# Hybrid decoder block on one core: the attention's scaling of probabilities moved in among the next unit's scores, one more bank for the first unit's transposes

## Chip, core and metric

The kernel runs on one core of one Trainium2 chip. The metric is the device time of one execution in microseconds (us); the median of three runs stands for a kernel. The trace and the profile page come from one further execution, taken by the hardware profiler.

## What is computed

One decoder layer over 512 tokens of width 1024, in float32: a pre-norm, one wide input projection, two mixers (a sparse-attention mixer with 8 query heads in 2 groups, and a recurrent mixer), gates, an output projection with a residual, and a gated feed-forward part. The change lies in the attention mixer alone. Its core is this, cut from the reference:

```python
q = rmsnorm(q.reshape(b, s, G, R, dh), q_norm_g) * (dh ** -0.5)      # G=2 groups, R=4 heads each, dh=64
s_c = einsum('bsgrd,bcgd->bgrsc', q, kc) + bias_c                    # compressed branch: 31 blocks
p_c = masked_softmax(s_c, dist_c >= 0);  o_cmp = einsum('bgrsc,bcgd->bsgrd', p_c, vc)
# selected branch (all blocks up to the token's own are chosen here) and window branch, each:
p = masked_softmax(einsum('bqgrd,bkgd->bgrqk', q, k) + bias, mask);  o = einsum('bgrqk,bkgd->bqgrd', p, v)
gt = sigmoid(gate)
o = gt[..., 0:1] * o_cmp + gt[..., 1:2] * o_slc + gt[..., 2:3] * o_win
```

## The kernel before

Ahead of the attention stage come the projections and the recurrent mixer, behind it the merge, the output projection and the feed-forward part. All dense products are float32 split into a high and a low part, three TensorE passes each (`whi` and `wlo` are the parts of a weight tile, 128x512 moving columns per matmul).

The attention stage works through twelve **units** `(qt, g, bs)`: a tile of 128 queries, a group of four heads, and one or both of the two branches. Units 0 to 3 are query tile 3 (512 keys a head), units 4 to 7 tile 2 (384 keys); each has one branch and four heads. Units 8, 9 (tile 1, 256 keys) and 10, 11 (tile 0, 128 keys) have both branches, so eight rows of scores. For each unit there are these steps:

- `scores(u, n)`: TensorE computes scores of the heads into the two PSUM banks of `pa()` (two matmuls a head, `KH` and `KL`), VectorE adds the bias, negates and takes the minimum on the way into SBUF tile `P` (line 1160, called a **read** below since it frees the bank), ScalarE takes the exponential in place and its sum into `sm`. Between the banks stand `n` **filler** matmuls of a dense projection (`filler`), which have nothing to do with the unit. At the end of the function stands the **scaling**: VectorE turns `sm` into gate over sum, and each head's `P` is multiplied by it, heads 0 to 2 on VectorE (`ts`), head 3 on ScalarE.
- `turns(u)`: groups of four 128x128 transposes of `P` on TensorE (line 1186) into a PSUM bank, called a **turn** here. Banks rotate: two of `pb()` and `tb3` (its tile name is `ps_mm`). `evac` copies each bank to `PTs`, turns with even numbers on ScalarE, odd ones on VectorE (line 1107).
- `compressed(qt)`: the compressed branch for a query tile: eight short matmuls into a `pa()` bank, softmax in `sC` on VectorE and ScalarE. `compressed_t(qt)` transposes `sC` (two transposes into a `pa()` bank, line 1138), ScalarE copies it back.
- `values(u)`: TensorE multiplies `sC` and `PTs` by the values into bank `Ob`, the bank of head sums; for the unit that completes a group ScalarE and VectorE split the result into `oaT`.

TensorE's order in this stage is the written one (`manual_schedule` for TensorE). The orders of VectorE and ScalarE are set by the scheduler of the tile framework when the kernel is built, those of GpSimd (POOL) and the DMA queue SP too. Every engine runs its own list in order, and an instruction that waits holds all behind it. The driving loop keeps scores two units ahead of the transposes:

```python
scores(units[0], 12); compressed(3); scores(units[1], 12)
for i, u in enumerate(units):
    turns(u)
    if i in (0, 4, 8, 10): compressed_t(u[0])
    if i + 2 < len(units): scores(units[i + 2], nfill[i])
    ...
    values(u)
```

Dense weights come by DMA, ScalarE makes `whi`, and in this stage GpSimd makes most `wlo` tiles (line 298, 128x512); a GpSimd subtraction starts when the filler's pass over the older `wlo` tile has ended.

Of the kernel before, what the change touches and what calls it, by code (L numbers as in the profile page):

```python
# [22 lines left out]
NT = S // 128  # L23
# [58 lines left out]
def hybrid_block(ctx: ExitStack, tc: tile.TileContext, A: dict, out: bass.AP):  # L82
# [25 lines left out]
    def bank(tag, bufs, shape=(128, 512)):  # L108
        return ps.tile(list(shape), F32, name="ps_" + tag, tag=tag, bufs=bufs)

    def mmb():
        return bank("mm", 4)

    def pa():
        return bank("a", 2)

    def pb():
        return bank("b", 2)

    def mm(o, l, r, start, stop):  # L120
        te.matmul(o, lhsT=l, rhs=r, start=start, stop=stop)  # L121

    def act(o, i, f=AF.Copy, **kw):
        sc.activation(o, i, f, **kw)  # L124

    def tt(o, a, b, op):
        v.tensor_tensor(o, a, b, op=op)  # L127

    def ts(o, a, s1, s2, op0=ALU.mult, op1=ALU.add):
        if s2 is None:  # L130
            v.tensor_scalar(o, a, s1, None, op0=op0)
        else:
            v.tensor_scalar(o, a, s1, s2, op0=op0, op1=op1)
# [25 lines left out]
    for name in ("rwkv_mu", "rwkv_w0", "rwkv_a0", "rwkv_k_k", "rwkv_k_a", "rwkv_r_k", "rwkv_ln_g", "rwkv_ln_b"):  # L159
        r0, n = ROWS[name]  # L160
# [46 lines left out]
    def norm_tiles(pool_):  # L207
        return (cp.tile([128, NT, 2], F32, name="ss", tag="ss"),
                [pool_.tile([128, D], F32, name="h", tag="h", bufs=NT) for _ in range(NT)])
# [101 lines left out]
    _, hs = norm_tiles(xp)  # L311
# [16 lines left out]
    with tc.manual_schedule(engines={getattr(mybir.EngineType, e) for e in ("PE", "Activation", "DVE", "Pool")}):  # L328
# [10 lines left out]
        for t in range(NT):  # L339
# [9 lines left out]
            if t == 1:  # L349
                pt = pts[7][:, 384:512]  # L350
# [5 lines left out]
        r0, n = ROWS["rwkv_mu"]  # L356
# [26 lines left out]
    def run(g):  # L383
        while True:
            try:
                next(g)
            except StopIteration as e:
                return e.value
# [226 lines left out]
    for k in range(31):  # L615
        m, n = 31 - k, k + 1
# [71 lines left out]
    pt = pa()  # L688
# [370 lines left out]
    Ob, db, tb3 = mmb(), [mmb(), mmb()], mmb()  # L1059
# [29 lines left out]
    def filler(n):  # L1089
        for _ in range(n):  # L1090
            next(fill, None)

    oaT = m2.tile([128, 2, NH2, S], F32R, name="oaT", tag="QK")
    ev, tn = [0], [0]
    Ps, PTk = {}, {}
# [5 lines left out]

    def evac(pt):
        PT = PTs[:, ev[0] % 8]
        if ev[0] % 2 == 0:
            act(PT, pt)
        else:
            v.tensor_copy(PT, pt)
        ev[0] += 1
        return PT

    def compressed(qt):
        qs = slice(128 * qt, 128 * qt + 128)
        pc = pa().rearrange("p (j g e a n) -> p j g e a n", j=2, g=2, e=2, a=2)
        for h in range(H):
            g, j, e = h // 4, h // 2 % 2, h % 2
            mm(pc[:, j, g, e], qst[:, h, qs], KC[:, g], True, True)
        sC = sC2[:, qt % 2]
        mx = at.tile([128, H], F32, name="mx", tag="mx", bufs=2)
        pcs = pc.rearrange("p j g e a n -> p (j g e) a n")
        tt(sC, pcs[:, :, 0], BC.rearrange("p j g e n -> p (j g e) n")[:, :, 24 - 8 * qt:56 - 8 * qt], ALU.add)  # L1120
        tt(sC, sC, pcs[:, :, 1], ALU.add)
        v.tensor_reduce(mx, sC, axis=AX.X, op=ALU.max)
        tt(sC, sC, mx[:, :, None].to_broadcast([128, H, 32]), ALU.subtract)
        act(sC, sC, AF.Exp)
        if qt == 0:
            tt(sC, sC, cmask[:, None, :].to_broadcast([128, H, 32]), ALU.mult)
        v.tensor_reduce(mx, sC, axis=AX.X, op=ALU.add)
        ts(mx, mx, 1e-30, None, op0=ALU.max)
        v.reciprocal(mx, mx)
        mxv = mx.rearrange("p (j g e) -> p j g e", j=2, g=2)  # L1130
        tt(mxv, mxv, gts[:, qt].rearrange("p (g j e x) -> p j g e x", g=2, j=2, e=2)[:, :, :, :, 0], ALU.mult)
        tt(sC, sC, mx[:, :, None].to_broadcast([128, H, 32]), ALU.mult)

    def compressed_t(qt):
        sC = sC2[:, qt % 2]
        pt = pa()
        for j in range(2):
            te.transpose(pt[:, 128 * j:128 * j + 128], sC[:, 4 * j:4 * j + 4].rearrange("p h n -> p (h n)"), ident)  # L1138
        act(sC.rearrange("p h n -> p (h n)"), pt[:, 0:256])

    def scores(u, n):
        qt, g, bs = u
        qs = slice(128 * qt, 128 * qt + 128)
        N = 128 * (qt + 1)
        R = 4 * len(bs)
        P = Pb[units.index(u) % 4][:, 0:R * N].rearrange("p (r n) -> p r n", n=N)
        nm = at.tile([128, 8], F32, name="nm", tag="nm", bufs=2)
        sm = at.tile([128, 8], F32, name="sm", tag="sm", bufs=2)
        per = 4 // (qt + 1)
        nb = R // per  # L1150
        for i0 in range(0, R, per):
            sp = pa()
            for i in range(i0, i0 + per):
                h, b = 4 * g + i % 4, bs[i // 4]
                o = sp[:, N * (i - i0):N * (i - i0) + N]
                mm(o, qst[:, h, qs], KH[:, b, g, 0:N], True, False)
                mm(o, qst[:, h, qs], KL[:, b, g, 0:N], False, True)
            for i in range(i0, i0 + per):
                h = 4 * g + i % 4
                v.tensor_tensor_reduce(out=P[:, i], in0=sp[:, N * (i - i0):N * (i - i0) + N], in1=BT[:, h, 384 - 128 * qt:512],  # L1160
                                       scale=-1.0, scalar=-NEG, op0=ALU.add, op1=ALU.min, accum_out=nm[:, i:i + 1])
                act(P[:, i], P[:, i], AF.Exp, scale=-1.0, bias=nm[:, i:i + 1], accum_out=sm[:, i:i + 1])
            ib = i0 // per
            filler(n * (ib + 1) // nb - n * ib // nb)
        v.reciprocal(sm[:, 0:R], sm[:, 0:R])
        for x, b in enumerate(bs):
            tt(sm[:, 4 * x:4 * x + 4], sm[:, 4 * x:4 * x + 4], gts[:, qt, 12 * g + 1 + b:12 * g + 12:3], ALU.mult)
        for i in range(R):
            if i % 4 == 3:
                act(P[:, i], P[:, i], AF.Copy, scale=sm[:, i:i + 1])  # L1170
            else:
                ts(P[:, i], P[:, i], sm[:, i:i + 1], None)
        Ps[u] = P

    def turns(u):
        qt, g, bs = u
        P = Ps.pop(u)
        PTk[u] = []  # L1180
        for x in range(len(bs)):
            for k in range(qt + 1):
                pt = tb3 if tn[0] % 3 == 2 else pb()
                tn[0] += 1
                for i in range(4):
                    te.transpose(pt[:, 128 * i:128 * i + 128], P[:, 4 * x + i, 128 * k:128 * k + 128], ident)  # L1186
                PTk[u].append((bs[x], k, evac(pt)))

    def values(u):
        qt, g, bs = u  # L1190
        qs = slice(128 * qt, 128 * qt + 128)
        O = Ob[:, 256 * g:256 * g + 256]
        if bs[0] == 0:
            sCT = sC2[:, qt % 2].rearrange("p h n -> p (h n)")
            for j in range(2):
                for e in range(2):
                    mm(O[64 * e:64 * e + 64, 128 * j:128 * j + 128], vcb[:, 2 * g + e], sCT[:, 128 * j:128 * j + 128],
                       j == 0, False)
        for b, k, PT in PTk.pop(u):
            for r in range(2):  # L1200
                mm(O[64 * r:64 * r + 64].rearrange("p (a q) -> p a q", a=2), vt[:, k, b, 64 * g:64 * g + 64],
                   PT.rearrange("p (h q) -> p h q", h=4)[:, r::2, :], False, b == 1 and k == qt)
        if bs[-1] == 1:
            ov = O.rearrange("p (a q) -> p a q", a=2)
            act(oaT[:, 0, 2 * g:2 * g + 2, qs], ov)
            tt(oaT[:, 1, 2 * g:2 * g + 2, qs], ov, oaT[:, 0, 2 * g:2 * g + 2, qs].bitcast(F32), ALU.subtract)

    units = [(qt, g, (b,)) for qt in (3, 2) for g in range(2) for b in range(2)]
    units += [(qt, g, (0, 1)) for qt in (1, 0) for g in range(2)]
    nfill = [5, 5, 6, 6, 7, 8, 10, 10, 10, 9, 9, 6]  # L1210
    with tc.manual_schedule(engines=KTS):
        scores(units[0], 12)
        compressed(3)
        scores(units[1], 12)
        for i, u in enumerate(units):
            turns(u)
            if i in (0, 4, 8, 10):
                compressed_t(u[0])
            if i + 2 < len(units):
                scores(units[i + 2], nfill[i])  # L1220
            else:
                filler(nfill[i])
            if i in (1, 5, 7):
                compressed({1: 2, 5: 1, 7: 0}[i])
            values(u)
        filler(100)
    dbg("oaT", oaT.bitcast(F32))
# [118 lines left out]
    for hf in range(2):  # L1346
        bo = dense_tok(512, aT[:, 0], aT[:, 1], NF)
        for t in range(NT):
            n = 256 if hf and t == NT - 1 else 512
# [32 lines left out]
```

## Time and profile before

| | |
|---|---|
| runs before (us) | 836.18, 836.18, 836.47; median 836.18 |
| profiled execution's own time | 836.53 us |
| its span, first to last instruction | 834.7 us |
| granted TensorE clock | 0.999 |
| attention stage in the trace | from 300.6 us (first score) to 397.3 us (last fillers) |
| busy over the span | TensorE 99%, VectorE 62%, ScalarE 49%, GpSimd 6% |

How to read it: "busy" of TensorE has modelled ends, so starts are compared with starts below. A row of the timeline reads: start in us, duration in us, engine, line, operation, written tile <- read tiles, shape, count, and in brackets how long the engine sat idle and who ended it. PE is TensorE, PEld its weight load, DVE VectorE, ACT ScalarE, POOL GpSimd. Lines are those of the kernel before.

### The profile page before, as it was taken

What the parts mean: (1) busy time and instruction counts of PE and PEld (TensorE: products, weight loads), DVE (VectorE), ACT (ScalarE), POOL (GpSimd) and SP (SyncE); (2) the same over time, 40 slices, a digit from 0 to 9 for tenths busy, and PEclk for the clock granted to TensorE, in tenths of its full rate; (3) what the DMA queues carried; (4) which work ended last, traced back from release to release, by engine and by line L of the source; (5) the groups of instructions that cost most, each with busy time, mean ns of one, the idle gap of its engine ahead of it and who ended that gap; (6) DMA issues with size and microseconds to landing.
All of it is one profiled execution on the core that took longest, in us unless ns stands there. A gap on an engine that the chain in (4) does not pass through costs nothing.

```text
span 834.7 us, 12900 instructions
## 1 busy us (share of the span) xinstructions
PE 824.0 (99%) x5107; PEld 669.6 (80%) x5107; DVE 515.7 (62%) x1004; ACT 406.7 (49%) x795; POOL 51.4 (6%) x67
## 2 busy tenths in 40 slices
PE   8999999999999999999999999999999999999998
PEld 7777778987777876777888988888888888888886
DVE  5577779964565878787665575566655566322222
ACT  6766655454455777676334454444444444221220
POOL 6100020140000110011000000000000000000000
PEclk9999999999999999999999999999999999999999
DMA  8432222246372310000275033333333332223421
GB/s 242 110 85 61 76 76 77 70 127 185 102 127 77 90 38 14 26 27 26 74 256 163 1 101 101 101 102 96 87 95 101 101 101 98 83 98 114 139 75 51
DMA packets 109400, 78.73 MB, mean 94 GB/s; under 512 B 3877, under 2 KB 98012, under 8 KB 109340
## 3 DMA queue, kind: packets, MB, share of 16 engines
q1 hardware_dynamic: 106800, 73.92, 31.0%
q10 hardware_dynamic: 1196, 2.55, 0.9%
q0 software_dynamic: 1344, 1.45, 0.8%
q8 instruction: 40, 0.66, 0.3%
q14 instruction: 20, 0.16, 0.1%
HBM read 74.56 MB, written 2.29 MB: 92 GB/s over the span
## 4 chain that ended last, share of the span: by engine, by line
PE 53%; DVE 0%; DVEq 0%; issue 0%
PE ps_mm L121 52%; PE ps_a L202 0%; PE ps_b L202 0%; PE ps_a L121 0%; PE ps_b L1186 0%; PE ps_mm L1186 0%; DVE x L127 0%; DVEq L1378 0%; PE ps_a L1138 0%
## 5 line engine op out<-in xcount | busy, mean ns | idle before, releaser
L298 DVE TENSOR_TENSOR wlo<-raw,whi 128x1024 fp32r<-128x1024 f32 (+1 forms) x111 | 131.4, 1185 | 184.4 <-PE ps_mm L121 160.0
L121 PE MATMUL ps_mm<-hh,whi 128*128 128x512 f32 (+1 forms) x624 | 242.4, 391 | 0.6 <-DVE hl L136 0.5
L121 PE MATMUL ps_mm<-hl,whi 128*128 128x512 f32 (+1 forms) x624 | 240.3, 387 | 0.0
L124 ACT ACTIVATE whi<-raw 128x1024 fp32r<-128x1024 f32 (+3 forms) x124 | 123.2, 995 | 159.2 <-PE ps_mm L121 143.4
L121 PE MATMUL ps_mm<-hh,wlo 128*128 128x512 f32 (+1 forms) x624 | 152.1, 384 | 0.0
L121 PEld LDWEIGHTS ps_mm<-hh,whi 128*128 128x128 f32 x624 | 117.3, 188 | 27.4 <-issue 1.0
L121 PEld LDWEIGHTS ps_mm<-hl,whi 128*128 128x128 f32 x624 | 117.3, 188 | 22.9 <-issue 1.0
L121 PEld LDWEIGHTS ps_mm<-hh,wlo 128*128 128x128 f32 x624 | 115.1, 188 | 23.5
L121 PE MATMUL ps_mm<-whi,aT 128*128 128x512 f32 x352 | 84.5, 390 | 0.0
L121 PEld LDWEIGHTS ps_mm<-whi,aT 128*128 128x128 f32 x352 | 65.9, 188 | 14.3 <-issue 0.4
L136 DVE SCALAR_TENSOR_TENSOR cgv<-ps_mm,cw,cgv 128x511 f32<-128x511 f32 (+1 forms) x88 | 65.4, 746 | 1.6
L124 ACT ACTIVATE cgv<-ps_mm,cw 128x512 f32<-128x512 f32 x44 | 34.2, 780 | 23.3 <-PE ps_mm L121 23.2
L121 PE MATMUL ps_mm<-wlo,aT 128*128 128x512 f32 x176 | 44.3, 389 | 0.0
L124 ACT ACTIVATE P<-P,nm 128x512 f32<-128x512 f32 (+3 forms) x64 | 35.3, 553 | 14.9 <-DVE nm L1160 14.9
L124 ACT ACTIVATE aT<-cgv 128x512 fp32r<-128x512 f32 x22 | 13.9, 631 | 56.8 <-DVE cgv L127 56.8
L121 PEld LDWEIGHTS ps_mm<-wlo,aT 128*128 128x128 f32 x176 | 33.0, 188 | 6.9
L124 ACT ACTIVATE cgv<-cgv 128x512 f32<-128x512 f32 x22 | 13.9, 632 | 41.3 <-DVE cgv L136 41.3
L298 POOL TENSOR_TENSOR wlo<-raw,whi 128x512 fp32r<-128x512 f32 (+3 forms) x13 | 20.5, 1573 | 203.5 <-PE ps_mm L121 134.0
L1160 DVE CUSTOM_DVE_ANT_0 P<-ps_a,AB 128x512 f32<-128x512 f32 (+3 forms) x64 | 29.4, 483 | 4.2 <-PE ps_a L121 3.7
L127 DVE TENSOR_TENSOR x<-x,ps_mm 128x512 f32<-128x512 f32 (+1 forms) x17 | 11.0, 654 | 24.1 <-PE ps_mm L121 22.7
L127 DVE TENSOR_TENSOR aT<-cgv,aT 128x512 fp32r<-128x512 f32 x22 | 15.2, 693 | 14.7 <-ACT aT L124 14.7
L124 ACT ACTIVATE QK<-ps_mm 128x64 f32<-128x64 f32 (+5 forms) x56 | 14.9, 310 | 18.3 <-PE ps_mm L121 18.2
(354 smaller groups left out, 1211.4 us busy)
## 6 DMA issues: line engine op xcount, KB each, us to landing
raw<-in_w_up_dram SPq DMA_DIRECT2D x44, 512.0 KB, 3.9
raw<-in_w_in_dram SPq DMA_DIRECT2D x38, 512.0 KB, 3.9
raw<-in_w_down_dram SPq DMA_DIRECT2D x22, 512.0 KB, 3.6
raw<-in_w_out_dram SPq DMA_DIRECT2D x8, 512.0 KB, 3.6
xt<-in_x_dram SPq DMA_DIRECT2D x4, 512.0 KB, 4.1
raw<-in_cmp_w_v_dram SPq DMA_DIRECT2D x4, 512.0 KB, 3.9
raw<-in_w_proj_b_dram SPq DMA_DIRECT2D x8, 256.0 KB, 2.7
raw<-in_w_proj_a_dram SPq DMA_DIRECT2D x8, 256.0 KB, 2.8
```

Of the source, the lines that this page charges most:

```text
L121: te.matmul(o, lhsT=l, rhs=r, start=start, stop=stop)
L124: sc.activation(o, i, f, **kw)
L127: v.tensor_tensor(o, a, b, op=op)
L136: v.scalar_tensor_tensor(o, a, s, b, op0=op0, op1=op1)
L298: eng.tensor_tensor(lo, raw, hi.bitcast(F32), op=ALU.subtract)
L1160: v.tensor_tensor_reduce(out=P[:, i], in0=sp[:, N * (i - i0):N * (i - i0) + N], in1=BT[:, h, 384 - 128 * qt:512], scale=-1.0, scalar=-NEG, ...
```

## The change

Four edits, all in the attention stage:

- **A bank**: the fourth turn of unit 0 (`tn[0] == 3`) goes into `Ob`, which nobody uses at that time; the later turns rotate as before, one place on (`tn[0] - (tn[0] > 3)`).
- **The compressed branch of tile 3**: `compressed(3)` is cut in two. It stops after the two additions that read the bank; the rest is issued after unit 0's turns. `compressed_t(3)` moves from right behind those turns to behind the first score bank of unit 2, and uses `tb3` and not a `pa()` bank.
- **Scaling**: a function of its own, `scale(u)`. For units 1 to 9 it is issued inside the `scores` of the next unit, behind its second bank (`mid`); for units 0, 10 and 11 it stays behind the unit's own scores. In the built program this lets VectorE take the next unit's reads between the multiplications of one unit.
- **Copies shared anew**: turns 3 (unit 0) and 27 (unit 7) are evacuated by ScalarE and not by VectorE; for tile 0 (units 10 and 11) all eight multiplications of a unit are on VectorE and none on ScalarE. 

The built programs show the same instructions in the same order on all engines outside this stage, and the same order on GpSimd and the DMA queue throughout. TensorE has the same instructions in the stage; its order differs at `compressed_t(3)` alone, beside the banks.

```diff
     def evac(pt):
         PT = PTs[:, ev[0] % 8]
-        if ev[0] % 2 == 0:
+        if ev[0] % 2 == 0 or ev[0] in (3,27):
             act(PT, pt)
...
         tt(sC, sC, pcs[:, :, 1], ALU.add)
+        if qt == NT - 1:
+            yield
...
     def compressed_t(qt):
-        pt = pa()
+        pt = tb3 if qt == NT - 1 else pa()
...
-    def scores(u, n):
+    def scores(u, n, mid=()):
...
             filler(n * (ib + 1) // nb - n * ib // nb)
+            if ib < len(mid):
+                mid[ib]()
+        Ps[u] = P, sm
+
+    def scale(u):
+        qt, g, bs = u
+        P, sm = Ps[u]
+        R = 4 * len(bs)
         v.reciprocal(sm[:, 0:R], sm[:, 0:R])
...
         for i in range(R):
-            if i % 4 == 3:
+            if i % 4 == 3 and qt:
                 act(P[:, i], P[:, i], AF.Copy, scale=sm[:, i:i + 1])
             else:
                 ts(P[:, i], P[:, i], sm[:, i:i + 1], None)
...
-                pt = tb3 if tn[0] % 3 == 2 else pb()
+                pt = Ob if tn[0] == 3 else tb3 if (tn[0] - (tn[0] > 3)) % 3 == 2 else pb()
...
+        behind = (1,2,3,4,5,6,7,8,9)
         scores(units[0], 12)
-        compressed(3)
+        scale(units[0])
+        comp = compressed(3)
+        next(comp)
         scores(units[1], 12)
         for i, u in enumerate(units):
             turns(u)
-            if i in (0, 4, 8, 10):
+            if i == 0:
+                run(comp)
+            if i in (4, 8, 10):
                 compressed_t(u[0])
             if i + 2 < len(units):
-                scores(units[i + 2], nfill[i])
+                mid = [lambda: None, functools.partial(scale, units[i + 1])] if i + 1 in behind else [lambda: None, lambda: None]
+                if i == 0:
+                    mid.insert(0, functools.partial(compressed_t, 3))
+                scores(units[i + 2], nfill[i], mid)
+                if i + 2 not in behind:
+                    scale(units[i + 2])
```

More of the change, by code (lines that the diff above doesn't have):

```diff
@@ L1 @@
+import functools
 import itertools
@@ L1172, in scores @@
                 ts(P[:, i], P[:, i], sm[:, i:i + 1], None)
-        Ps[u] = P
     def turns(u):
         qt, g, bs = u
-        P = Ps.pop(u)
+        P, _ = Ps.pop(u)
         PTk[u] = []
@@ L1223, in hybrid_block @@
             if i in (1, 5, 7):
-                compressed({1: 2, 5: 1, 7: 0}[i])
+                run(compressed({1: 2, 5: 1, 7: 0}[i]))
             values(u)
```

## Prediction, made before the changed kernel ran

> **What bounds the kernel now.** I read the page first, then the busy time by stretches, then TensorE's timeline through the attention stage, and last VectorE, ScalarE and GpSimd at each place where TensorE waits.
>
> ```profile
> PE 824.0 (99%) x5107; PEld 669.6 (80%) x5107; DVE 515.7 (62%) x1004; ACT 406.7 (49%) x795; POOL 51.4 (6%) x67
> 476.33 354.54 PE ps_mm L121 x1584
> 300.60:397.30 96.70, 93.44 (x647) 72.41 (x645) 79.01 (x278) 68.77 (x192) 10.30 (x8) 1.00 0.08 23
> 312.50:318.80 6.30, 4.89 (x26) 3.10 (x24) 6.09 (x18) 5.04 (x13) 0.62 (x1) 1.00 0.14 42
> ```
>
> TensorE is busy 99%. The second line, a piece of the chain of waits, is TensorE alone for the last 354.54 us: what the attention stage gains or loses arrives at the end one to one. The change removes no TensorE work (same instructions, one order altered), so it can only move TensorE's idle time. The third line is the stage (length, then busy time of PE, PEld, DVE, ACT, POOL): 96.70 - 93.44 = 3.26 us idle. The fourth shows where most lies: 6.30 - 4.89 = 1.41 us around unit 0's turns, where VectorE is busy 6.09 of 6.30 us. Ends are modelled, so idle time is understated; below I compare starts.
>
> **Place A, units 0 to 2: a gain of 1.28 us.** TensorE, then GpSimd and VectorE:
>
> ```profile
> 311.55 1.03 PE L1186 MATMUL ps_b<-kc,P 128*128 128x128 f32 x8
> 312.42 0.60 PE L1186 MATMUL ps_mm<-kc,P 128*128 128x128 f32 x4
> 313.80 0.66 PE L1186 MATMUL ps_b<-kc,P 128*128 128x128 f32 x4 [0.78 <-DVE PTs L1107]
> 314.57 0.44 PE L1138 MATMUL ps_a<-kc,sC 128*128 128x128 f32 x2
> 315.54 0.44 PE L121 MATMUL ps_a<-KH,qst 128*128 128x512 f32 x1
> 316.96 0.50 PE L121 MATMUL ps_a<-KH,qst 128*128 128x512 f32 x1 [0.52 <-DVE nm L1160]
> 318.78 0.66 PE L121 MATMUL ps_mm<-sC,kc 128*64 128x128 f32 x8
> ...
> 311.85 1.28 POOL L298 TENSOR_TENSOR wlo<-raw,whi 128x512 fp32r<-128x512 f32 x1 [9.54 <-ACT sC L124]
> 312.23 0.92 DVE L131 TENSOR_SCALAR mx<-mx 128x8 f32<-128x8 f32 x1
> 314.09 0.42 DVE L127 TENSOR_TENSOR sC<-sC,mx 128x256 f32<-128x256 f32 x1
> 314.43 1.27 DVE L131 TENSOR_SCALAR P<-P,sm 128x512 f32<-128x512 f32 x3
> 316.22 0.68 DVE L1160 CUSTOM_DVE_ANT_0 P<-ps_a,AB 128x512 f32<-128x512 f32 x1
> ...
> 331.83 0.16 DVE L131 TENSOR_SCALAR mx<-mx 128x8 f32<-128x8 f32 x1
> ```
>
> Eight transposes take 312.42 - 311.55 = 0.87 us, a turn 0.44. The fourth turn should start at 312.86 and starts at 313.80: it waits for a bank that VectorE (line 1107) has to copy. In `Ob` it waits for nothing, and the turns end at 313.29. Two transposes and a score bank with its filler take 0.97 (314.57 to 315.54), the bank alone so 0.77. It comes first now, and the transposes of `sC` are wanted at 314.06. `sC` isn't ready: its 128x8 step on VectorE took 0.92 us where the same form took 0.16 at 331.83, and ended at 313.15, with GpSimd's 311.85 + 1.28 = 313.13. Nothing in the change moves that, nor the copy behind it; `sC` is final at about 314.46 as before. So the transposes start at 314.5: 0.94 of wait goes, 0.45 comes. Transposes and second bank, 0.97, and 0.1 of restart (the first matmul after a wait lasts 0.50, as at 316.96, where an estimated 0.4 is usual) end at 315.57. The third bank needs VectorE's first read of unit 2. Before, that stood behind three multiplications (1.27 from 314.43) and a copy, at 316.22, and TensorE waited to 316.96. In the new order one multiplication (0.42) and the two small steps on `sm` (0.2) stand ahead: read from 314.97, done 315.65, third bank at 315.68. The way from there to `values` is unchanged, 318.78 - 316.96 = 1.82: 317.50, against 318.78. Bounds: 0.9 if the read comes 0.4 later, 1.73 if `sC` comes when wanted.
>
> The two edits that leave ScalarE one copy more (turn 3, 0.6 us) are free: it copies three banks until 314.6, before `sC` wants it at 314.7. Without that cover the bank `tb3` would go back 0.6 us later, with `values` behind it.
>
> **Place B, units 3 and 4: 0.48 us of it are given back.**
>
> ```profile
> 338.01 0.66 PE L1186 MATMUL ps_b<-kc,P 128*128 128x128 f32 x4
> 332.28 1.29 POOL L298 TENSOR_TENSOR wlo<-raw,whi 128x512 fp32r<-128x512 f32 x1 [19.16 <-PE ps_mm L121]
> 332.92 0.68 DVE L127 TENSOR_TENSOR mx<-mx,gts 128x8 f32<-128x8 f32 x1
> 333.52 0.68 DVE L136 SCALAR_TENSOR_TENSOR AB<-AB,ps_mm 128x512 f32<-128x512 f32 x1
> 334.45 0.55 DVE L1160 CUSTOM_DVE_ANT_0 P<-ps_a,AB 128x384 f32<-128x384 f32 x1
> 336.86 0.62 ACT L124 ACTIVATE P<-P,sm 128x384 f32<-128x384 f32 x1 [0.51 <-DVE sm L127]
> 337.38 0.58 ACT L124 ACTIVATE PTs<-ps_b 128x512 f32<-128x512 f32 x1
> ```
>
> Unit 3's fourth turn (338.01) waits for ScalarE's copy of its first turn (337.38). That stands behind the multiplication of unit 4's head 3 (336.86), and so behind all four reads of unit 4, the third of them at 334.45. This chain doesn't come forward by the whole 1.28 us. GpSimd's span moves with TensorE, to about 331.1 to 332.4; the last step on `sC` (two inputs in SBUF) and the filler step of 0.6 (333.52) are in line before the third read. A step of that kind ran until GpSimd's end at 332.92 (0.68, to 333.60; GpSimd ended at 333.57). So: step on `sC` done 332.7, filler step 333.3, one multiplication of unit 3 that the edit puts here, 0.36, 333.66, third read there: 0.79 earlier than before, with an unchanged tail behind it. TensorE leaves the fourth turn 0.8 us ahead, whatever it was ahead before: a loss of 0.48. Bounds: 0.3 ahead if the step on `mx` too loses to GpSimd (I place it 0.1 us before GpSimd's start); 1.4 if neither waits.
>
> [...]
>
> **Place C, unit 9: a gain of 0.97 us.**
>
> ```profile
> 365.37 1.67 DVE L131 TENSOR_SCALAR P<-P,sm 128x256 f32<-128x256 f32 x6
> 366.95 1.28 DVE L1107 COPY PTs<-ps_b 128x512 f32<-128x512 f32 x2
> 368.15 0.41 DVE L1160 CUSTOM_DVE_ANT_0 P<-ps_a,AB 128x256 f32<-128x256 f32 x1
> 367.33 1.29 POOL L298 TENSOR_TENSOR wlo<-raw,whi 128x512 fp32r<-128x512 f32 x1 [10.96 <-PE ps_mm L121]
> 367.74 0.86 PE L121 MATMUL ps_mm<-obT,whi 128*128 128x512 f32 x3
> 368.97 0.39 PE L121 MATMUL ps_a<-KH,qst 128*128 128x256 f32 x1 [0.37 <-DVE nm L1160]
> 370.26 0.38 PE L121 MATMUL ps_a<-KH,qst 128*128 128x256 f32 x1
> ```
>
> Three fillers from 367.74 end their turn at 368.44, and TensorE starts at 368.97: 0.53 plus 0.1 of restart. The next wait is 0.35 long: 368.97 to 370.26 is 1.29, and four score matmuls at about 0.12 and two fillers at 0.23 make 0.94. VectorE is late: six multiplications and two copies stand before unit 9's first read at 368.15. New, one copy is ScalarE's (turn 27, 0.6) and the sixth multiplication comes behind four reads (0.28). With TensorE 0.8 us ahead the read starts at about 366.6 and is not missed. The fifth multiplication starts at 366.33, GpSimd at 366.5: a margin of 0.2 us.
>
> **Places D and E, units 8 and 9: -0.40 and +0.75 us.**
>
> ```profile
> 373.89 0.66 PE L1186 MATMUL ps_b<-kc,P 128*128 128x128 f32 x4
> 373.64 0.91 ACT L124 ACTIVATE P<-P,sm 128x256 f32<-128x256 f32 x2 [0.17 <-DVE sm L127]
> 374.46 0.36 ACT L124 ACTIVATE oaT<-ps_mm 128x256 fp32r<-128x256 f32 x1
> 374.72 1.33 ACT L124 ACTIVATE PTs<-ps_b 128x512 f32<-128x512 f32 x2
> 375.95 0.41 ACT L124 ACTIVATE sC<-sC 128x256 f32<-128x256 f32 x1
> 383.06 1.04 PE L1186 MATMUL ps_b<-kc,P 128*128 128x128 f32 x8
> 384.89 0.66 PE L1186 MATMUL ps_mm<-kc,P 128*128 128x128 f32 x4 [0.79 <-ACT PTs L124]
> 383.39 0.69 ACT L124 ACTIVATE P<-P,sm 128x128 f32<-128x128 f32 x2 [0.53 <-DVE sm L127]
> 384.25 0.59 ACT L124 ACTIVATE PTs<-ps_mm 128x512 f32<-128x512 f32 x1
> ```
>
> D: unit 8's fourth turn waits for ScalarE's copy of the first. Before, the copy began 0.83 us after the turns (373.89 to 374.72). In the new order ScalarE does `oaT` first, which can start only when `values` of unit 7 ends, 0.1 after the turns begin; then one multiplication (0.45) and the `sC` exponential (0.41), moved ahead; then the copy: 0.1 + 0.26 + 0.45 + 0.41 = 1.2, so 0.4 later. E: unit 9's fourth turn should start at 383.06 + 0.87 = 383.93 and starts at 384.89, 0.96 late: ScalarE copies only at 384.25, behind the two multiplications of unit 10 at 383.39. Those are VectorE's now; ScalarE is free for the copy when unit 10's exponentials end, and 0.2 us of wait are left. The two multiplications cost VectorE 0.4 us more in units 10 and 11, hidden: its next read is wanted 1 us later.
>
> The sum in time saved: 1.28 - 0.48 + 0.97 - 0.40 + 0.75 = 2.1 us. The profiled execution took 836.53, so 834.4 for its like; the median of the runs is 0.35 lower, 836.18, and gives **834.1 us**. No DMA or GpSimd order changes, and the loads have slack in the stage (share 0.08).
>
> **Rivals.** (1) *More is kept* (0.2): places B and D don't bind, because the copies on ScalarE come early enough. Speaks for it that one small step decides B. Then 2.1 + 0.48 + 0.40 = 3.0: 833.2. (2) *The fourth turns eat it* (0.22): each unit of four turns has three banks, so TensorE ahead only waits longer for ScalarE's copy, at C as well as at B; rows 338.01 and 384.89 are such waits already. What is left is the 0.8 at B and about 0.1 behind it, 0.9: 835.3. (3) *The edit does nothing*, the scheduler placing the multiplications where they were: the built order speaks against it, so it has no share of its own beside (2). (4) *Slower* (0.1): multiplications among the reads meet GpSimd's spans (332.28, 367.33, in unit 10 one more of 1.3) and hold the reads queued behind them. The point: a VectorE step in SBUF starting after GpSimd does, 0.1 us later in unit 4, 0.2 in unit 9. Each costs up to 1.3; all three, 3.9, against the 2.1 + 0.7 (B with no wait on `sC`, 1.4 against 0.8) of gain otherwise: 1.1 worse, 837.3.
>
> **How the numbers follow.** The forecast has 0.48. A measurement of this kernel can tell about 0.2% (1.67 us) from no change, so 834.5 is the border of faster. The forecast lies 0.4 beyond it, and its B and D are each uncertain by some 0.5: seven tenths of it (0.34), and all of (1) (0.2), give faster 0.54. Slower by over 0.2% (above 837.85) needs (4) with a further wait, 0.05. The rest, 0.41, is within. The range 832.6 to 836.1 takes in (1) with A's upper bound, and (2) with B's lower one, and leaves (4) out.
>
> **What would show it.** Right: no wait at unit 0's fourth turn; `sC` transposes at about 314.5; unit 3's fourth turn near 337.1 behind ScalarE's copy; no wait for a read in unit 9; the last fillers of the stage 2.1 us earlier. Wrong: VectorE multiplications of over 1 us ending with a GpSimd subtraction and a TensorE wait for a read behind them; or stage gain lost after 397 us.

## The result, and the profile after

The kernel after the change takes **833.82 us** (median of 8 runs, 833.71 to 834.27), against 836.30 us for the kernel before in the same session (836.18 to 836.58): 2.48 us less, a ratio of 0.9971 with a 95% interval of 0.9961 to 0.9980. The profiled execution took 833.78 us with a span of 831.9 us. In the listings of after, lines 121, 124, 127, 131, 136, 298, 1107, 1138, 1160 and 1186 of before are 122, 125, 128, 132, 137, 299, 1108, 1141, 1163 and 1196; in the versions with GpSimd's pieces the lines behind 299 stand two further down.

First the page's busy time, then the busy time by stretches (length, then busy time of PE, PEld, DVE, ACT, POOL; granted clock, DMA share, GB/s):

```profile
PE 823.2 (99%) x5107; PEld 669.9 (81%) x5107; DVE 514.4 (62%) x1006; ACT 406.4 (49%) x793; POOL 51.5 (6%) x67
300.60:395.00 94.40, 92.68 (x646) 72.58 (x645) 77.94 (x280) 68.65 (x190) 10.49 (x8) 1.00 0.09 25
312.50:318.80 6.30, 5.83 (x40) 3.94 (x40) 5.38 (x18) 6.01 (x15) 0.18 (x1) 1.00 0.14 42
```

No engine's busy time has changed by more than 1.3 us. Over the stage TensorE is idle 94.40 - 92.68 = 1.72 us where it was idle 3.26, and in the stretch around unit 0's turns 6.30 - 5.83 = 0.47 us where it was idle 1.41. Three of the four waits that the profile lists for TensorE between 305 and 398 us (engine, tile, line, what it waited for; total us, how often, longest):

```profile
PE ps_mm L1196 <- ACT PTs L125: 0.6, 1, 0.6
PE ps_mm L1141 <- DVE sm L128: 0.5, 1, 0.5
PE ps_b L1196 <- ACT PTs L125: 0.2, 1, 0.2
```

These are the three waits that the prediction left or added: unit 3's fourth turn, the transposes of `sC`, and unit 8's fourth turn. The fourth, 0.2 us for `sC` at a score bank, stood in before as well. The waits for reads of unit 2 and unit 9 are gone, and so is the one at unit 9's fourth turn. TensorE's timeline at the places A, B, C, D and E, in this order:

```profile
311.10 1.03 PE L1196 MATMUL ps_b<-kc,P 128*128 128x128 f32 x8
311.97 1.04 PE L1196 MATMUL ps_mm<-kc,P 128*128 128x128 f32 x8
314.18 0.41 PE L1141 MATMUL ps_mm<-kc,sC 128*128 128x128 f32 x2 [0.46 <-DVE sm L128]
315.29 0.50 PE L122 MATMUL ps_a<-KH,qst 128*128 128x512 f32 x1
336.69 0.55 PE L1196 MATMUL ps_mm<-kc,P 128*128 128x128 f32 x3 [0.58 <-ACT PTs L125]
366.46 0.86 PE L122 MATMUL ps_mm<-obT,whi 128*128 128x512 f32 x3
367.16 0.28 PE L122 MATMUL ps_a<-KH,qst 128*128 128x256 f32 x1
368.15 0.39 PE L122 MATMUL ps_a<-KH,qst 128*128 128x256 f32 x1
371.78 1.09 PE L1196 MATMUL ps_b<-kc,P 128*128 128x128 f32 x8
373.53 0.65 PE L1196 MATMUL ps_b<-kc,P 128*128 128x128 f32 x4 [0.22 <-ACT PTs L125]
381.67 1.07 PE L1196 MATMUL ps_b<-kc,P 128*128 128x128 f32 x8
```

One thing must be taken out before the two traces are compared. Unit 0's first turn starts at 311.10, and at 311.55 before: 0.45 us earlier, though up to there TensorE has the same instructions in the same order. The 0.45 us are there already at 212 us, long before the stage. So every later start of after has 0.45 us that the change didn't give. What it gave is the *lead*: a start in before, less the same start in after, less 0.45. The lead, read at the first turns of units 1, 4, 8, 9 and 10, grows by 1.21 at A (up to unit 1), -0.41 at B (from unit 1 to unit 4), 0.86 at C (to unit 8), -0.28 at D (to unit 9) and 0.98 at E (to unit 10); a plus is time gained. That is 2.36 us in all, against 2.48 in the medians.

The same was worked out for each kernel below, each with its own start of unit 0's first turn. "Behind E" is what the lead changes by behind unit 10's first turn. The last column is its median less that of before in its own session, so there a minus is time gained.

| kernel | A | B | C | D | E | behind E | sum | measured |
|---|---|---|---|---|---|---|---|---|
| after | 1.21 | -0.41 | 0.86 | -0.28 | 0.98 | 0 | 2.36 | -2.48 |
| bank undone | 0.83 | -0.42 | 0.84 | -0.27 | 0.98 | 0 | 1.97 | -1.95 |
| bank alone | -0.08 | -0.08 | -0.01 | 0.01 | -0.01 | 0 | -0.17 | +0.18 |
| `sC` transposed at the old place | 0.67 | -0.41 | 0.88 | -0.28 | 0.98 | 0 | 1.84 | -1.87 |
| no scaling among scores | 0.56 | -0.09 | 0.60 | -0.01 | 0.98 | 0 | 2.05 | -1.97 |
| turn 27 back on VectorE | 1.21 | -0.42 | 0.48 | -0.02 | 0.98 | 0 | 2.24 | -2.19 |
| ScalarE's multiplications kept | 1.20 | -0.43 | 0.86 | -0.27 | 0.96 | 0 | 2.33 | -2.35 |
| no scaling, ScalarE's kept | 0.52 | -0.10 | 0.61 | -0.02 | -0.01 | 0 | 1.01 | -1.16 |
| the same, turn 27 back too | 0.55 | -0.09 | -0.01 | 0.01 | -0.01 | 0 | 0.46 | -0.49 |
| after, GpSimd in two pieces | 1.76 | 0.14 | 0.87 | -0.28 | 0.98 | 0 | 3.48 | -3.15 |
| before, GpSimd in two pieces | 0.43 | 0.20 | 0.01 | -0.01 | 0.42 | 0 | 1.05 | -1.00 |
| four pieces, `sC` in `Ob` | 1.62 | -0.02 | 1.27 | -0.27 | 0.98 | -0.48 | 3.10 | -3.18 |
| the same, unit 9 on VectorE | 1.62 | -0.02 | 1.27 | 0.12 | 0.98 | -1.01 | 2.96 | -2.99 |

In twelve of the thirteen rows sum and measurement agree within 0.15 us; in the other, after with GpSimd in two pieces, 0.33 us stays open. The intervals of the ratios reach about 0.001 to each side, 0.8 us, so it is the traces that tell such small edits apart: each is read from the column of its place. There is one trace for each kernel, but in the columns that an edit leaves alone the kernels agree within 0.03 us (B, C, D and E of the bank undone and of `sC` at the old place, against after).

### The profile page after: what moved, and what is told of

It reads as the page before. It is cut to its first block, busy times and chain, and to the rows that moved or that the text cites. A ratio compares the mean times of both kernels' runs of the same rounds, so it can differ in the third digit from the quotient of the medians.

```text
span 831.9 us, 12894 instructions
## 1 busy us (share of the span) xinstructions
PE 823.2 (99%) x5107; PEld 669.9 (81%) x5107; DVE 514.4 (62%) x1006; ACT 406.4 (49%) x793; POOL 51.5 (6%) x67
## 3 DMA queue, kind: packets, MB, share of 16 engines
q10 hardware_dynamic: 1196, 2.55, 0.9%
## 4 chain that ended last, share of the span: by engine, by line
PE 91%; DVE 5%; ACT 2%; issue 1%; DMA 0%; DVEq 0%; ACTq 0%
PE ps_mm L122 81%; PE ps_a L122 5%; PE ps_b L122 2%; PE ps_b L1196 1%; PE ps_mm L1196 1%; DVE AB L128 0%; DMA xt<-in_x_dram 0%; DVE P L1163 0%; DVE sC L128 0%; DVE wlo L299 0%; ACT P L125 0%; ACT L125 0%; ACT UV L125 0%; DVE P L132 0%; DVE PTs L1108 0%
```

## The experiments

**The bank, undone in after and done alone in before.**

```diff
-                pt = Ob if tn[0] == 3 else tb3 if (tn[0] - (tn[0] > 3)) % 3 == 2 else pb()
+                pt = tb3 if (tn[0] - (tn[0] > 3)) % 3 == 2 else pb()
```

> The kernel after, but unit 0's fourth transposes go to the rotating bank that the second pool would give, not to Ob. My theory: the fourth turn again waits about 0.6 us for the copy of the first bank, but the transposes of sC cannot start before about 314.2 in any case, so the wait lies inside one that stays. What is lost is only that the third score bank, and with it the first read of unit 2, comes some 0.4 us later: about +0.4 us against after (834.2). Rival: the whole wait that before had there, 0.94 us, counts: +0.9 us (834.75). Second rival: nothing, because the sC wait covers all of it: 0 to 0.1 us.

> The kernel before, with the bank alone: unit 0's fourth transposes in Ob, nothing else moved. My theory: the fourth turn no longer waits and the four turns end near 313.3, but the sC transposes and the third score bank are set by VectorE, whose list is unchanged (three multiplications and a copy ahead of unit 2's first read), so TensorE only waits later: 0 against before, within 0.2 us (836.3). Rival: the 0.94 us of wait at the fourth turn is gained in full: 835.4.

Undone: 834.29 us, ratio 0.9976 (0.9966 to 0.9986). Alone: 836.42 us, ratio 1.0002 (0.9993 to 1.0011). TensorE with the bank undone, then with the bank alone:

```profile
313.57 0.66 PE L1196 MATMUL ps_b<-kc,P 128*128 128x128 f32 x4 [0.98 <-DVE PTs L1108]
314.76 0.38 PE L1141 MATMUL ps_mm<-kc,sC 128*128 128x128 f32 x2
```
```profile
312.48 1.04 PE L1186 MATMUL ps_mm<-kc,P 128*128 128x128 f32 x8
315.11 0.44 PE L1138 MATMUL ps_a<-kc,sC 128*128 128x128 f32 x2 [1.59 <-DVE sC L127]
```

Undone, the fourth turn waits 0.98 us (0.6 was expected), but the transposes of `sC` then wait for nothing, and place A loses only 0.38 us. (VectorE's order changes with it, two multiplications and not one ahead of unit 2's first read; but TensorE runs without a gap from 313.57 to the third score bank at 315.70, so its own delay is enough for the loss.) Alone, the fourth turn doesn't wait, and the time comes back as a wait of 1.59 us for `sC`, ahead of which VectorE now copies a bank; the third score bank of unit 2, which needs VectorE's first read, starts at 317.10, where it was 316.96. So the bank's wait was worth nothing by itself, and 0.4 us once the order behind it was mended. Both rivals that counted the wait in full fail, and so does the one that gave the bank nothing in after.

**The transposes of `sC` back behind unit 0's turns.**

```diff
-            if i in (4, 8, 10):
+            if i in (0, 4, 8, 10):
                 compressed_t(u[0])
...
-                if i == 0:
-                    mid.insert(0, functools.partial(compressed_t, 3))
```

The transposes use a `pa()` bank again.

> The kernel after, but the two transposes of the first unit's sC stand directly behind the turns again (bank of the score pool), not behind the first score bank of unit 2. My theory: TensorE, in order, waits at them until sC is final, with no score bank to fill that time: the first score bank starts about 0.5 us later and everything behind it too: +0.5 to +0.6 us against after (834.3 to 834.4). Rival: the third bank waits for VectorE's read anyway, so the place of the transposes changes nothing: 0.

834.37 us, ratio 0.9977 (0.9969 to 0.9986): 0.61 us more than after by the medians (each taken against before in its own session), 0.52 by the lead, all of it at A. TensorE in this kernel:

```profile
314.15 0.44 PE L1141 MATMUL ps_a<-kc,sC 128*128 128x128 f32 x2 [1.08 <-DVE sC L128]
```

The transposes wait 1.08 us, from the end of the turns on, and no score bank fills that time.

**No scaling among the next unit's scores.**

```diff
-        behind = (1,2,3,4,5,6,7,8,9)
+        behind = ()
...
         scores(units[1], 12)
+        scale(units[1])
```

> The kernel after, but no unit's probabilities are scaled among the next unit's scores: each unit's multiplications stand behind its own scores, as before the change. The bank, the place of the sC steps and the copies' sharing stay as after. My theory: at place A about 0.7 us are lost again (VectorE's multiplications stand ahead of unit 2's first read), at place C 0.85 to 1.0 us; at places B and D, where the change gave time back, 0.3 to 0.5 us are regained in part: in sum +1.0 to +1.5 us against after (834.8 to 835.3). Rival: the scaling's place is what carries nothing and the bank and copies do it all: 0 to +0.3 us. [...]

834.27 us, ratio 0.9976 (0.9965 to 0.9986): 0.3 us more by the lead, 0.5 by the medians, not 1.0 to 1.5. Against after, A loses 0.65 (expected 0.7), B and D give back 0.32 and 0.27 (expected 0.3 to 0.5 in part). C was the miss: it loses 0.26 and not 0.85 or more. VectorE at unit 9 in this kernel:

```profile
364.58 1.67 DVE L132 TENSOR_SCALAR P<-P,sm 128x256 f32<-128x256 f32 x6
366.17 0.68 DVE L1108 COPY PTs<-ps_b 128x512 f32<-128x512 f32 x1
366.77 0.41 DVE L1163 CUSTOM_DVE_ANT_0 P<-ps_a,AB 128x256 f32<-128x256 f32 x1
```

All six multiplications stand ahead of the read, but only one copy does, since turn 27 is ScalarE's. The two edits overlap at C.

**Turn 27's copy, and ScalarE's multiplications in units 10 and 11, each undone in after.**

```diff
-        if ev[0] % 2 == 0 or ev[0] in (3,27):
+        if ev[0] % 2 == 0 or ev[0] == 3:
```
```diff
-            if i % 4 == 3 and qt:
+            if i % 4 == 3:
```

> The kernel after, but the copy of turn 27 (unit 8) is VectorE's again, as before; the order written by the scheduler moves VectorE's last multiplications of unit 8 by one. Theory: VectorE is later at unit 9's reads by 0.6 us less what is moved behind them, and the reads had only 0.02 to 0.3 us of margin: +0.2 to +0.4 us against after (834.0 to 834.2). Rival, that VectorE has slack there: 0. Rival on the other side: ScalarE, relieved, copies unit 8's first bank 0.5 us earlier and the fourth turn's wait of 0.3 goes: -0.2 us.

> The kernel after, but ScalarE keeps one of four multiplications in the last four units (qt 0: two in each) as before; VectorE does the rest. Theory from the trace after: unit 10's exponentials end at 379.88 and ScalarE then stands idle until 380.86, so two multiplications of 0.3 us fit in front of its copy; the gain at unit 9's fourth turn came from unit 10's reads no longer being held by GpSimd: 0 to +0.1 us against after (833.8 to 833.9). Rival, step E of the prediction: the multiplications on ScalarE delay the copy of the first bank: +0.7 us (834.5).

(Turn 27 belongs to unit 7; the text on record names the wrong unit in its bracket.) Turn 27 undone: 834.24 us, ratio 0.9974 (0.9963 to 0.9984). C loses 0.38 us, and D, where ScalarE is relieved, gains 0.26, so the first theory and the second rival are both there and nearly cancel. ScalarE's multiplications kept: 834.08 us, ratio 0.9972 (0.9962 to 0.9983). The lead at E stays at 0.96, so the rival, which is step E of the prediction, fails.

**Two edits undone together, then three.** What is one edit's work, when either of two will do, shows only with both undone. The diffs are those above.

> The kernel after with two edits undone: no probabilities scaled among the next unit's scores, and ScalarE again does one multiplication of four in the last units. Each undone alone left the gain at unit 9's fourth turn (0.98 us of lead between unit 9's and unit 10's turns) whole. Theory: either is enough, since the copy of unit 9's first bank is late only where GpSimd holds unit 10's reads AND two multiplications stand ahead of the copy on ScalarE. Then with both undone the gain at that place is gone (0 to 0.2 us of lead instead of 0.98) and the time is 0.8 to 1.0 us over that of the kernel without scaling among scores (834.27), 835.1 to 835.3. Rival, that the gain has a third cause: 834.3.

> As the run with both undone, and turn 27's copy on VectorE again: of the change only the bank, the place of the first unit's sC steps and turn 3's copy are left. Theory: at unit 9's reads the copy moved to ScalarE and the moved multiplications each make VectorE early enough for most of it, so the 0.61 us of lead gained there without the multiplications falls to 0 to 0.2 us: some 0.4 to 0.6 us slower than the run with two edits undone, 835.6 to 835.9. Rival, that the lead there comes from place A and not from either edit: no slower.

Two: 835.13 us, ratio 0.9986 (0.9977 to 0.9994), and the gain at E is gone (-0.01). Three: 835.80 us, ratio 0.9994 (0.9985 to 1.0003), and that at C is gone too (-0.01, from 0.61). Both came as expected. E in the rows of five kernels: where it is shown, GpSimd and VectorE's step of `mx` or `sC` that meets it, then ScalarE, then TensorE. Before (its rows of ScalarE and TensorE stand in the prediction):

```profile
377.96 1.28 POOL L298 TENSOR_TENSOR wlo<-raw,whi 128x512 fp32r<-128x512 f32 x1 [9.34 <-PE ps_mm L121]
378.18 1.09 DVE L131 TENSOR_SCALAR mx<-mx 128x8 f32<-128x8 f32 x1
```

After:

```profile
376.13 1.48 POOL L299 TENSOR_TENSOR wlo<-raw,whi 128x512 fp32r<-128x512 f32 x1 [8.77 <-PE ps_mm L122]
376.05 0.42 DVE L128 TENSOR_TENSOR sC<-sC,mx 128x256 f32<-128x256 f32 x1
379.88 0.19 ACT L125 ACTIVATION_READ_ACCUMULATOR P<-P,nm 128x1 f32 x1
380.86 0.38 ACT L125 ACTIVATE oaT<-ps_mm 128x256 fp32r<-128x256 f32 x1 [0.80 <-PE ps_mm L122]
```

After with ScalarE's multiplications kept:

```profile
380.72 0.70 ACT L125 ACTIVATE P<-P,sm 128x128 f32<-128x128 f32 x2 [0.53 <-DVE sm L128]
381.59 0.59 ACT L125 ACTIVATE PTs<-ps_b 128x512 f32<-128x512 f32 x1
381.79 1.09 PE L1196 MATMUL ps_b<-kc,P 128*128 128x128 f32 x8
```

After without scaling among scores:

```profile
376.58 1.27 POOL L299 TENSOR_TENSOR wlo<-raw,whi 128x512 fp32r<-128x512 f32 x1 [8.74 <-PE ps_mm L122]
376.79 1.08 DVE L132 TENSOR_SCALAR mx<-mx 128x8 f32<-128x8 f32 x1
381.88 0.60 ACT L125 ACTIVATE PTs<-ps_b 128x512 f32<-128x512 f32 x1
```

Both edits undone:

```profile
376.62 1.09 DVE L132 TENSOR_SCALAR mx<-mx 128x8 f32<-128x8 f32 x1
381.84 0.70 ACT L125 ACTIVATE P<-P,sm 128x128 f32<-128x128 f32 x2 [0.53 <-DVE sm L128]
382.70 1.07 ACT L125 ACTIVATE PTs<-ps_b 128x512 f32<-128x512 f32 x2
383.34 0.66 PE L1196 MATMUL ps_b<-kc,P 128*128 128x128 f32 x4 [0.79 <-ACT PTs L125]
```

In before the step of eight columns takes 1.09 us, to 379.27, with GpSimd's end at 379.24, and unit 10's later reads stand behind it (the next one at 379.18). With the scaling moved, VectorE is past its steps on `mx` when GpSimd starts (the last began at 375.70), unit 10's reads are not held (the first four, from 376.38 to 377.29 beside GpSimd, took 0.28 or 0.29 us each), and ScalarE is idle for 0.80 us before `oaT`: its two multiplications fit in there. Without it, VectorE's step of eight columns takes 1.08 us and the exponentials end late; but when the multiplications are VectorE's, the copy still comes in time. Only where the hold and the multiplications come together is the copy late, and the wait of 0.79 us that before had is back.

**GpSimd's subtractions in pieces.** Only GpSimd's own list changes: each 128x512 subtraction becomes two of 128x256.

```diff
-            eng.tensor_tensor(lo, raw, hi.bitcast(F32), op=ALU.subtract)
+            cuts = (slice(0, kt // 2), slice(kt // 2, kt)) if eng is nc.gpsimd and kt == NH2 else (slice(0, kt),)
+            for c in cuts:
+                eng.tensor_tensor(lo[:, c], raw[:, c], hi[:, c].bitcast(F32), op=ALU.subtract)
```

> The kernel after, with one thing changed: each of GpSimd's 128x512 subtractions (wlo from raw and whi, 1.28 us each) is cut in two of 128x256, back to back; only GpSimd's own list differs. Theory that GpSimd holds a VectorE step with two inputs in SBUF until its instruction ends: the step gets in at half the span, so the hold of sC at place A (mx step 0.80 us) shrinks by about 0.5 and that of sC<-sC,mx at place B (1.13 us) by about 0.5 too, and the gain is about 0.8 us against after (833.0, between 832.7 and 833.6). Rival, that the long VectorE steps and GpSimd's ends only coincide (a common releaser): 0, with the mx step still at 0.8 us.

> The kernel before with the same cut of GpSimd's 128x512 subtractions in two halves. Lock theory: sC of the first unit comes 0.3 to 0.5 us earlier, the 128x8 step at unit 10 (1.09 us before) ends at half the span and ScalarE's exponentials and multiplications of unit 10 with it, so that the wait at unit 9's fourth turn shrinks by about 0.5: 0.5 to 1.2 us less than before (835.1 to 835.8). Rival: 0.

In after: 833.28 us, ratio 0.9961 (0.9949 to 0.9974). In before: 835.43 us, ratio 0.9988 (0.9979 to 0.9997). The holds, first in after as it is, then in after with two pieces (places A and B in each):

```profile
311.40 1.28 POOL L299 TENSOR_TENSOR wlo<-raw,whi 128x512 fp32r<-128x512 f32 x1 [9.54 <-ACT sC L125]
311.90 0.80 DVE L132 TENSOR_SCALAR mx<-mx 128x8 f32<-128x8 f32 x1
330.64 1.29 POOL L299 TENSOR_TENSOR wlo<-raw,whi 128x512 fp32r<-128x512 f32 x1 [17.96 <-PE ps_mm L122]
331.09 1.13 DVE L128 TENSOR_TENSOR sC<-sC,mx 128x256 f32<-128x256 f32 x1
```
```profile
312.00 1.42 POOL L301 TENSOR_TENSOR wlo<-raw,whi 128x256 fp32r<-128x256 f32 x2 [9.39 <-ACT sC L125]
312.52 0.25 DVE L132 TENSOR_SCALAR mx<-mx 128x8 f32<-128x8 f32 x1
331.14 0.57 DVE L128 TENSOR_TENSOR sC<-sC,mx 128x256 f32<-128x256 f32 x1
```

(The theory of both texts is about a hold that the trace of before shows: the steps at 312.23 and 332.92 took 0.92 and 0.68 us, where 0.16 is usual for each, and ended within 0.03 us of GpSimd's instruction.) The held steps fall from 0.80 to 0.25 us and from 1.13 to 0.57. The lead grows by 0.55 at A and 0.55 at B and nowhere else; in before it grows by 0.43 at A, 0.20 at B and 0.42 at E. So the long steps were no coincidence: with GpSimd's instruction cut in two they became shorter by 0.55 and 0.56 us, and the rival fails. Of the 0.8 us that were expected in after the medians show 0.67 (3.15 against 2.48), the lead 1.12.

**Two versions meant to be the best.** GpSimd in four pieces, and the `sC` of units 4, 8 and 10 transposed into `Ob`; then unit 9's two ScalarE multiplications on VectorE as well.

```diff
-        pt = tb3 if qt == NT - 1 else pa()
+        pt = tb3 if qt == NT - 1 else Ob
```
```diff
-            if i % 4 == 3 and qt:
+            if i % 4 == 3 and qt and u != units[9]:
```

> The kernel after, GpSimd's 128x512 subtractions cut in four of 128x128, and the transposes of sC for units 4, 8 and 10 in Ob instead of the score banks. Against the version cut in two (833.28): a hold ends at a quarter of the span and not at half, 0.1 to 0.2 us at places A and B together; the wait of 0.32 us for ScalarE's copy of sC at unit 4's second score bank goes. Sum 0.3 to 0.5: 832.8 to 833.0. Rival: GpSimd's four pieces take so much longer in all that its transfers or VectorE come late: over 833.3.

> The version before this one in the list (GpSimd in four pieces, sC transposed into Ob), with unit 9's two ScalarE multiplications moved to VectorE, so that ScalarE's copy of unit 8's first bank stands in front of them: the wait at unit 8's fourth turn (0.38 us over the usual step) goes, VectorE is 0.5 us later in unit 10, where ScalarE had 0.8 us idle behind the exponentials. 0.2 to 0.4 us less: 832.4 to 832.7. Rival: VectorE's two extra multiplications push unit 10's exponentials back by more than the 0.8 and the wait comes back at unit 9's fourth turn: 0 or slower.

833.11 us, ratio 0.9961 (0.9948 to 0.9973), and 833.30 us, ratio 0.9962 (0.9950 to 0.9975): the medians are within 0.2 us of that with two pieces alone, and the leads are smaller (3.10 and 2.96 against 3.48). Neither gained what was expected. The wait at unit 4's second bank did go (C is 1.27 in place of 0.86), and the wait at D went in the second (0.12 and not -0.27). But `Ob` has a price in unit 10. TensorE in the first, then VectorE and TensorE in the second:

```profile
388.97 0.44 PE L1143 MATMUL ps_mm<-kc,sC 128*128 128x128 f32 x2 [0.25 <-DVE mpad L1257]
```
```profile
387.21 1.66 DVE L132 TENSOR_SCALAR P<-P,sm 128x128 f32<-128x128 f32 x8
388.78 0.42 DVE L128 TENSOR_TENSOR oaT<-ps_mm,oaT 128x256 fp32r<-128x256 f32 x1
389.26 0.44 PE L1143 MATMUL ps_mm<-kc,sC 128*128 128x128 f32 x2 [0.78 <-DVE mpad L1257]
```

There `Ob` still holds unit 9's sums until VectorE has read them into `oaT`, behind eight multiplications. (The `mpad` that the row names only came last before it.) That costs 0.48 and 1.01 us by the starts behind it. And four pieces are no better than two: the step at B took 0.57 us beside two pieces and 0.72 beside four. A version with two pieces and `Ob` for unit 4 alone follows from these columns, some 0.4 us below two pieces; it was not run.

## Why the prediction was right, point by point

The forecast of 834.1 us was 0.3 us from the measured 833.82, and where its sum was 2.1 us the lead shows 2.36. The misses of the single steps, 0.07 to 0.23 us, cancel in part. By its steps, in the order of the sum:

- **A, 1.28: measured 1.21.** As described: no wait at the fourth turn, the transposes at 314.18 (314.63 on before's clock; 314.5 was said), held by `sC`, with the 128x8 step at 0.80 us again ending with GpSimd (312.70 and 312.68). The third bank is at 315.29, with 0.45 added 315.74, where 315.68 was said. The experiments show that no edit does it by itself: with the bank alone it is -0.08, without the bank 0.83, without the scaling 0.56. No run undid turn 3's copy on ScalarE, or the cut of `compressed(3)`, by itself; that the copy is free stays the prediction's argument.
- **B, -0.48: measured -0.41.** The wait for ScalarE's copy stands (the turn came at 336.69, with 0.45 added 337.14, near 337.1 as said), and the chain behind it is the one named. The step on `mx`, which decided between the bounds, began 0.11 us before GpSimd (330.53 and 330.64) where 0.1 was said. The step on `sC` was held until 332.22, with 0.45 added 332.67, said 332.7; the third read came at 333.13, with 0.45 added 333.58, said 333.66:

```profile
333.13 0.54 DVE L1163 CUSTOM_DVE_ANT_0 P<-ps_a,AB 128x384 f32<-128x384 f32 x1
336.06 0.58 ACT L125 ACTIVATE PTs<-ps_mm 128x512 f32<-128x512 f32 x1
```

  Cutting GpSimd's instruction turns the -0.41 into 0.14; in before the same cut gives 0.20 there, so the change then costs 0.06 at B, which shows the hold as the cause. One clause does not hold: that TensorE leaves this turn 0.8 us ahead "whatever it was ahead before". With 1.21, 0.83 and 0.67 gained at A, B took -0.41, -0.42 and -0.41: the loss is fixed, and not the lead, because GpSimd's start moves with TensorE (1.19 us earlier in after, from unit 0's first turn; for the other two an estimate from their leads). With A's size right, both come to 0.8.
- **C, 0.97: measured 0.86.** The reads are not waited for, as said. Two terms were a little large: the step from 366.46 to 367.16 (0.70) was 1.23 before, so 0.53 without the 0.1 of restart that was added, and that from 367.16 to 368.15 (0.99) was 1.29, so 0.30 and not 0.35. What the prediction took as two parts of one sum, 0.6 from the copy and 0.28 from the multiplications, overlap: 0.60 remains with the copy alone, 0.48 with the multiplications alone, nothing with neither.
- **D, -0.40: measured -0.28.** ScalarE did what was said:

```profile
371.90 0.38 ACT L125 ACTIVATE oaT<-ps_mm 128x256 fp32r<-128x256 f32 x1 [0.53 <-PE ps_mm L122]
372.18 0.51 ACT L125 ACTIVATE P<-P,sm 128x256 f32<-128x256 f32 x1
372.58 0.41 ACT L125 ACTIVATE sC<-sC 128x256 f32<-128x256 f32 x1
372.88 0.59 ACT L125 ACTIVATE PTs<-ps_b 128x512 f32<-128x512 f32 x1
```

  The copy starts 1.10 us after the turns and not 1.2. The term that was too large is the exponential: its 0.41 is a duration, and from its start to the next start it is 0.30.
- **E, 0.75: measured 0.98, and not for the reason given alone.** This is the step that failed. The gain was put down to the two multiplications taken from ScalarE, with 0.2 us of wait left; kept on ScalarE, they cost 0.02, and no wait is left. In after the hold of unit 10's reads, which stood in the trace of before at the same place, is gone by the moved scaling, and ScalarE has 0.80 us to spare. The two edits are each enough (the rows above): the prediction saw one of the two causes and missed the other, and the size came out near by luck. The margin was small: VectorE's step on `sC` began only 0.08 us before GpSimd here (376.05 and 376.13), and the same step, 0.45 us behind GpSimd's start at B, was held (1.13 us).

Rival 1 named the right side (more is kept) but not the place: B and D bind. Rival 2 fails: the fourth turns took 0.41 and 0.28, whatever TensorE was ahead, and not C as well. Rival 3, that the multiplications stay where they were, fails with the run without scaling, which loses 0.31 of the lead. Rival 4, GpSimd holding the multiplications for up to 1.3 us each, did not come up, and no run shows such a hold. In unit 9 the read behind them began as GpSimd did:

```profile
366.06 1.30 POOL L299 TENSOR_TENSOR wlo<-raw,whi 128x512 fp32r<-128x512 f32 x1 [10.93 <-PE ps_mm L122]
366.04 0.42 DVE L1163 CUSTOM_DVE_ANT_0 P<-ps_a,AB 128x256 f32<-128x256 f32 x1
```

In unit 4 the moved multiplication came when GpSimd was done (332.74 and 331.93). The trace therefore doesn't show whether such a multiplication would be held; the in-place step of 128x8, the same operation, was (0.80 us, where 0.16 is usual). In the version with four pieces and `Ob` for three units, one multiplication began at 331.92, 0.22 us before the last piece ended, and took 0.50 us, where 0.48 is usual: too little to tell.

## What to carry to other kernels

A wait that the profile names is worth what is left after the next wait in line: here 0.94 us at one bank was worth nothing alone and 0.4 with the order behind it mended, so the reading has to go on to the next step that isn't ready. When several edits relieve one place, undo them together as well as singly: singly, ScalarE's multiplications and the moved scaling cost 0.02 us and nothing at E, and together 0.99. And a step of a few columns that takes five times its usual time (here 0.80 us in after and 0.92 in before, where 0.16 is usual) is worth a look at GpSimd, where cutting its instruction in two gave 1.1 us by the lead and 0.67 by the medians, where undoing any one of the edits lost 0.5 and 0.6 at most.

## What the runs showed of the hardware

- VectorE's step on `mx` of 128x8 (in place, in SBUF) and its step on `sC` with two inputs in SBUF began 0.50 and 0.45 us behind GpSimd's start in after and were held to about GpSimd's end: they took 0.80 and 1.13 us beside one instruction of 1.28 and 1.29, and ended at 312.70 and 332.22, GpSimd at 312.68 and 331.93. The hold was not for GpSimd's whole list: beside two halves they took 0.25 and 0.57 us and ended at 312.77 and 331.71, GpSimd's second half at 313.42 and 332.32.
- At E it was GpSimd that took longer. Where VectorE's step on `sC` began 0.08 us before GpSimd (376.05 and 376.13), that step took its usual 0.42 us and GpSimd 1.48 in place of 1.28: 0.20 more, where the step had 0.34 left. With ScalarE's multiplications kept it was the same: 0.08 us before GpSimd (376.17 and 376.25), 0.42 and 1.49 us.
- A reciprocal of 128x8 took 0.20 us at 312.80 in after with two pieces, where GpSimd ran until 313.42, as it did at 312.74 in after, 0.06 us behind GpSimd's end: this step in SBUF was not held.
- Two halves took 1.42 us in all at A and 1.62 at B. Four quarters took 1.71 us at A, from 311.41, and the step on `mx` 0.40 us beside them, to 312.31; with equal quarters, an estimate, the second ended at 312.27. At B they took 1.90 us, from 330.24 to 332.14, and the step on `sC` 0.72 us, from 330.68 to 331.40; where the quarters end there was not shown. So these held steps too ended before GpSimd's list did, and that a step waits for the piece that runs when it comes is an estimate from A.
- Profiled executions of the same order stood up to 0.5 us apart at unit 0's first turn (0.45 us earlier than before in after, 0.06 later with the bank alone), so leads of a stage are to be taken from the stage's own start.
